# A hybrid decoder layer on one core: the sums over scale 2 and half of shift 2 move from the tensor engine to GpSimd

## The chip, the core and the metric

The kernel runs on one core of a Trainium2 chip. The core has a tensor engine (PE) for matrix products, VectorE (DVE) and ScalarE (ACT) for elementwise work, GpSimd (POOL), and a queue engine (SP) that here issues the loads. The engines run side by side, each through its own list of instructions in a fixed order, and wait for one another by semaphores. The metric is the device time of one execution in microseconds (us).

## The reference

One layer over 256 tokens of width 2048. A conditioning vector c gives six modulations through one large matrix; four token mixers share an input projection and an output projection; a gated feed-forward with a short convolution follows.

```python
cond = jax.nn.silu(c)
mod = (cond @ w_mod[l] + b_mod[l]).reshape(B, 6, D)
sh1, sc1, g1, sh2, sc2, g2 = [mod[:, i, None, :] for i in range(6)]

h = rmsnorm(x, norm_mix[l]) * (1.0 + sc1) + sh1
proj = f32(h @ w_in[l])
...
y = jnp.concatenate([y_a, y_b, y_c, y_d], axis=-1).astype(x.dtype) @ w_out[l]
x = x + g1 * y

h = rmsnorm(x, norm_ffn[l]) * (1.0 + sc2) + sh2
x = x + g2 * conv_ffn(h, ffn_w_gate[l], ffn_w_up[l], ffn_conv_w[l], ffn_conv_b[l], ffn_w_down[l])
```

The four mixers y_a to y_d are gated linear attention, gated DeltaNet, multi-scale pooling and forgetting attention. The change concerns the product `cond @ w_mod` for sc2 and the first half of sh2: a vector of 2048 times a 2048 x 1024 block of w_mod, three times.

## The kernel before

All is float32. A weight is loaded as a tile `wr` of 128x1024 (512 KB), split by ScalarE into a high part `wh` (L115) and by VectorE into a low part `wl` (L100, the difference), and the tensor engine makes three products of high and low parts where one full-precision product stands in the reference.

The modulations are matrix times vector, so they are made differently. w_mod is 2048 rows high; a load brings 128 rows of 1024 columns into a tile `wm`. There are 16 loads for each block of 1024 columns, a "job". The function `gemv` (L174) sums them in one of two ways:

- on VectorE: one instruction (L103) multiplies wm by the column of `cond` that belongs to the rows and adds into `ga`, 128x1024. After 16 loads, a product with a column of ones adds up the 128 partitions.
- on the tensor engine (`pst` is given): the column of `cond`, repeated over 32 columns, is the stationary operand, and wm streams through it in two halves of 512 (L193). Two loads and two halves fill four strips of 32 columns side by side, in one PSUM bank `bgt`. ScalarE copies the bank into a buffer of the tag wr (L201), and a product with `sel`, which holds ones in the rows 0 and 64, or 32 and 96, picks and adds the strips.

`gemv` is a generator: it yields after each two loads, a "step". L53 and L54 say which job goes which way: "s0 s1 h0" (both halves of scale 2, the first of shift 2) on the tensor engine, "h1 g0 g1" (the second half of shift 2, both halves of gate 1) on VectorE.

The stages around this are, in order:

- The modulations sh1 and sc1 and the input projection, in four groups of K tiles (to L527). The last group leaves 25 visits to pairs of column tiles (`extras`, L470).
- The mixers, with these last visits in between. At each visit, `paced` (L908) advances the tensor engine's jobs by 0.38 of a step and VectorE's by 0.69. So the loads of w_in and the loads of w_mod alternate. After the mixers' instructions, what is left of the jobs is written out, first those of the tensor engine, then those of VectorE (L940 to L943).
- The output projection (`project`, L950), which loads w_out, multiplies by gate 1 (`g1t`) and adds the residual.
- The second norm; scale 2 `s2` and shift 2 `sh2` enter at L1007. Then the feed-forward half (to L1088), where gate 2 is summed on VectorE as well.

The last step of a gate 1 job waits, in the order of writing, until the tensor engine's jobs are written out (L487). The buffers that the jobs share are four tiles of wm, whoever sums them; five of wr; and one bank bgt.

The code gives a priority by its order of writing; a planner puts the instructions of each engine in a fixed order, by this priority and its own estimate of when each can run, and within it the loads of SP. A load for which no buffer is free holds all loads behind it on SP. GpSimd runs few instructions: memsets (`ga` at L179, `Sg` at L813), twelve comparisons for masks (L393), and small powers for norms (L320, L577, L726, L839, L998, L1079).

Of the kernel before, what the change touches and what calls it, by code (L numbers as in the profile page):

```python
# [16 lines left out]
P = 128  # L17
# [11 lines left out]
# columns of w_in  # L29
# [3 lines left out]
# columns of the constant array  # L33
# [23 lines left out]
def _consts():  # L57
    i = np.arange(P)
    s, t = i[:, None], i[None, :]
    same = (s // CH) == (t // CH)  # L60
    cols = [s == t, same & (s <= t), same & (s > t), s <= t, np.ones((P, P)), s > t]
    cols.append(np.where(t > s, -1e30, 0.0))
    for w in (2, 4, 8, 16):
        cols.append(np.broadcast_to(1.0 / np.minimum(np.arange(1, 17), w), (P, 16)))
    # the level at which s and t part, counted from 1 above the diagonal and from 7 below it
    lv = sum((l + 1) * ((s // (2 * m) == t // (2 * m)) & (s % (2 * m) < m) & (t % (2 * m) >= m))
             for l, m in enumerate(LEVELS))
    lw = lv.T
    cols.append(lv + np.where(lw > 0, lw + len(LEVELS), 0))
    return np.ascontiguousarray(np.concatenate([np.asarray(a, np.float32) for a in cols], axis=1))  # L70
# [3 lines left out]
def trunk_kernel(ctx: ExitStack, tc: tile.TileContext, x, c, w_mod, b_mod, norm_mix, norm_ffn, w_in,  # L74
# [18 lines left out]
    def kt_(shape, name, dt=F32):  # L93
        return keep.tile(shape, dt, name=name, tag=name)
# [71 lines left out]
    last_wm = [None]  # L166
# [7 lines left out]
    def gemv(col0, done, pst=None, ready=lambda: True, bias=None):  # L174
        """cond * w over 1024 columns: without pst summed by partition on VectorE, else on the tensor engine,
        four column tiles side by side"""
        acc = pst() if pst else keep.tile([P, 1024], F32, name="ga", tag="ga")
        if bias is not None:
            G.memset(acc, 0.0)  # L179
            nc.sync.dma_start(acc[0:1], bias)  # L180
        for k in range(0, KT, 2):
            wms = []
            for kk in range(2):
                wms.append(wp.tile([P, 1024], F32, name="wm", tag="wm", bufs=4))
                last_wm[0] = nc.sync.dma_start(wms[kk], wm_v[:, k + kk, col0:col0 + 1024])
            for kk in range(2):
                wm = wms[kk]
                if not pst:
                    accumulate(acc, wm, k + kk, bias is None)
                    continue  # L190
                for c in range(2):
                    o = 64 * kk + 32 * c
                    mm(acc[o:o + 32], cond[:, k + kk:k + kk + 1].to_broadcast([P, 32]), wm[:, c * 512:c * 512 + 512],  # L193
                       start=k == 0, stop=k == KT - 2)
            if k == KT - 2:
                while not ready():
                    yield
                with tc.high_priority():
                    if pst:
                        gr = wp.tile([P, 1024], F32, name="wr", tag="wr", bufs=5)[:, 0:512]  # L200
                        S_.copy(gr, acc)  # L201
# [25 lines left out]
    # ================= attention half =================  # L227
    with ExitStack() as ph:
# [11 lines left out]
        # projections: gla q 0:2, k 2:4, g 4:8, gdn g 8:12, pool 12:16, fox q 16:20, k 20:24  # L240
# [16 lines left out]
        def gates():  # L257
# [13 lines left out]
            # columns 0:4 1/(1+e), columns 4:12 1/(2+e)  # L271
# [16 lines left out]
        with ExitStack() as st:  # L288
# [25 lines left out]
            # 1 + b_mod of the two scales  # L314
# [19 lines left out]
            # sh1, sc1 of the K tiles of group g, then h  # L334
# [60 lines left out]
            # the small columns: lr 0:16, b 16:20, a 20:24, f 24:28; row 28 is one  # L395
# [30 lines left out]
            # one pair of column tiles over some groups of K tiles; two sums share a bank: only the first clears it  # L426
# [49 lines left out]
            def jobs(seq, pst):  # L476
                col = pst or (ext)
                for job in seq.split():
                    kind, n = job[0], int(job[1])
                    k0, col0 = 8 * n, dict(s=4, h=3, g=2)[kind] * D + n * 1024  # L480
                    if kind == "s":
                        yield from gemv(col0, to_col(s2, 4, k0, nffn, col), pst)
                    elif kind == "h":
                        yield from gemv(col0, to_col(sh2, 3, k0, None, col), pst)
                    else:
                        yield from gemv(col0, g1_row(n, bgt), None,
                                        lambda: "gf"[n] in emitted and "s" in emitted, b_mod[:, col0:col0 + 1024])  # L487
# [7 lines left out]
            # g1 takes the place of values no longer needed  # L495
# [10 lines left out]
            bg = [marked(jobs(ON_PE, bgt)), jobs(ON_DVE, None)]  # L506
# [22 lines left out]
            # conv of gdn's q, k, v straight from the accumulators  # L529
# [16 lines left out]
        bgp = ph.enter_context(tc.tile_pool(name="bgp", bufs=1, space=PSUM))  # L546
        mx = ph.enter_context(ExitStack())
# [19 lines left out]
        def gated_deltanet():  # L567
            # norms of q and k
# [12 lines left out]
            # decays within the chunk  # L581
# [28 lines left out]
                # -M^T (and its diagonal, which no level takes)  # L610
# [9 lines left out]
            # inverse of I + M by blocks of 2, 4, .. 64: X = inverse, Y = its transpose  # L620
# [42 lines left out]
                # attention [j, i]  # L663
# [5 lines left out]
                # queries times the decay from the chunk's start  # L669
# [6 lines left out]
            # u and w^T, over the values' and the keys' place  # L676
# [10 lines left out]
            # the states, chunk by chunk, over M and X  # L687
# [34 lines left out]
                # r = c * (c^2 * ss / d + eps)^-1/2  # L722
# [17 lines left out]
        def gla(lp):  # L740
# [4 lines left out]
            # log decays by token, then their sums within the chunk by feature  # L745
# [14 lines left out]
            # attention within the chunk, [s, t], heads by parity: the diagonal, then level by level  # L760
# [29 lines left out]
            # to and from the states  # L790
# [16 lines left out]
            for cc in range(NC - 1):  # L807
# [4 lines left out]
                s = lt([P, 2, 256], "Sg", bufs=3)  # L812
# [93 lines left out]
        rate, owed = (PE_RATE, DVE_RATE), [0.0, 0.0]  # L906
# [81 lines left out]
    # ================= feed-forward half =================  # L988
    with ExitStack() as ph:
# [3 lines left out]
        with tc.tile_pool(name="hp", bufs=2, reuse_waits="tile") as hp:  # L993
# [7 lines left out]
            # transposed and scaled by the norm in one product  # L1001
# [12 lines left out]
        def proj(gp, view, c0):  # L1014
            """four column tiles, weights stationary: [features, tokens], the high and the low part's sums side by side"""
# [29 lines left out]
        # down: tokens stationary; g2 and the final norm's weight by row  # L1045
# [72 lines left out]
```

## Time and profile before

| | us |
|---|---|
| median of 3 runs | 1316.04 |
| lowest and highest run | 1313.96 and 1318.38 |
| span of the profiled execution, first to last instruction | 1312.4 |
| PE busy in it | 1257.7 |
| VectorE busy | 886.8 |
| ScalarE busy | 640.7 |
| GpSimd busy | 23.1 |

The profile is one execution; the page gives its span and no other time for it. The slices of the span, a fortieth each, show how the stages follow:

```profile
PE   2799999999999999899999999999999999999996
DVE  7688797989763497456656665665666587974553
POOL 0200000010000100000000000000000000000000
DMA  9999998796567996345565565555655699875552
```

Each digit is the busy share in tenths. The mixers lie in the slices 8 to 14, the output projection in 14 to 17; from there on it is the feed-forward half. A busy PE says little of how much it does: the ends of matmuls are modelled, and a matmul counts as busy while it passes through the array.

### The profile page before, as it was taken

To read this page: it belongs to the slowest core of one execution; us is meant where nothing else is said; L and a number is where in the kernel's file an instruction comes from. 1 tells how busy PE (TensorE), PEld (TensorE's weight loads), DVE (VectorE), ACT (ScalarE), POOL (GpSimd) and SP (SyncE) were. 2 spreads that over 40 slices of the span, in tenths; PEclk is the share of its full clock that TensorE was granted. 3 is DMA by queue.
4 is the path that set the end of the run, shared out by engine and by line. 5 is a ranking of instruction groups with operands and counts; after the bars stand their busy time and mean duration, and the time that the engine had idled before them with its cause. 6 is when DMAs were issued, how large, how long until landed. Compare 5 with 4: busy or idle time off the path is not lost.

```text
span 1312.4 us, 20435 instructions
## 1 busy us (share of the span) xinstructions
PE 1257.7 (96%) x7955; PEld 1100.5 (84%) x7955; DVE 886.8 (68%) x1185; ACT 640.7 (49%) x1008; POOL 23.1 (2%) x31
## 2 busy tenths in 40 slices
PE   2799999999999999899999999999999999999996
PEld 1799999898876788888888888888888888888896
DVE  7688797989763497456656665665666587974553
ACT  3455344674364444465545455554555454443432
POOL 0200000010000100000000000000000000000000
PEclk8799999999999999899999999999999999999998
DMA  9999998796567996345565565555655699875552
GB/s 332 287 368 376 312 353 279 259 334 211 176 233 247 328 338 230 125 161 186 170 206 180 189 190 183 190 184 187 191 184 172 206 356 378 304 260 188 192 182 81
DMA packets 174232, 311.95 MB, mean 238 GB/s; under 512 B 16172, under 2 KB 65331, under 8 KB 173495
## 3 DMA queue, kind: packets, MB, share of 16 engines
q1 hardware_dynamic: 174135, 310.65, 70.3%
q8 instruction: 62, 1.02, 0.3%
q14 instruction: 35, 0.29, 0.1%
HBM read 308.51 MB, written 2.10 MB: 237 GB/s over the span
## 4 chain that ended last, share of the span: by engine, by line
PE 91%; DMA 4%; DVE 1%; SPq 1%; ACT 1%; issue 1%; POOLq 0%; POOL 0%; ACTq 0%; DVEq 0%
PE fpt L97 57%; PE ext L97 15%; PE wot L97 5%; PE acc L97 4%; PE gdt L97 4%; PE bgt L97 3%; DMA wm<-in_w_mod_dram 3%; PE oxt L97 2%; DMA wr<-in_w_in_dram 1%; DMA wr<-in_w_out_dram 1%; DVE ga L103 1%; DVE wl L100 0%; ACT h L112 0%; SPq L155 0%; SPq L399 0%
## 5 line engine op out<-in xcount | busy, mean ns | idle before, releaser
L100 DVE TENSOR_TENSOR wl<-wr,wh 128x1024 fp32r<-128x1024 f32 x384 | 468.5, 1223 | 299.7 <-ACT wh L115 298.8
L115 ACT CAST wh<-wr 128x1024 fp32r<-128x1024 f32 x384 | 402.4, 1051 | 497.5 <-PE fpt L97 315.5
L97 PE MATMUL fpt<-bigA,wh 128*128 128x512 f32 x1408 | 485.0, 397 | 0.7 <-ACT h L112 0.7
L97 PE MATMUL fpt<-bigA,wl 128*128 128x256 f32 x1408 | 375.2, 281 | 0.0
L97 PEld LDWEIGHTS fpt<-bigA,wh 128*128 128x128 f32 x1408 | 260.9, 188 | 60.7 <-ACT h L112 0.9
L97 PEld LDWEIGHTS fpt<-bigA,wl 128*128 128x128 f32 x1408 | 259.5, 188 | 5.0
L103 DVE SCALAR_TENSOR_TENSOR ga<-wm,cond,ga 128x1024 f32<-128x1024 f32 x139 | 177.9, 1280 | 9.9 <-DMA wm<-in_w_mod_dram 8.7
L97 PE MATMUL fpt<-wl,AH 128*128 128x512 f32 (+1 forms) x440 | 152.9, 348 | 0.0
L97 PE MATMUL fpt<-wh,AL 128*128 128x512 f32 (+1 forms) x440 | 152.5, 347 | 0.0
L97 PE MATMUL fpt<-wh,AH 128*128 128x512 f32 (+1 forms) x440 | 142.6, 348 | 0.0
L97 PE MATMUL ext<-bigA,wh 128*128 128x256 f32 x768 | 137.9, 281 | 0.0
L97 PEld LDWEIGHTS ext<-bigA,wh 128*128 128x128 f32 x768 | 117.8, 189 | 3.1 <-DVE dS L100 0.8
L97 PE MATMUL ext<-bigA,wl 128*128 128x256 f32 x384 | 107.6, 281 | 1.7 <-DVE wl L100 1.7
L97 PEld LDWEIGHTS fpt<-wh,AH 128*128 128x128 f32 x440 | 83.3, 189 | 10.9 <-ACT wh L115 0.2
L97 PEld LDWEIGHTS fpt<-wh,AL 128*128 128x128 f32 x440 | 83.3, 189 | 10.5 <-issue 0.2
L97 PEld LDWEIGHTS fpt<-wl,AH 128*128 128x128 f32 x440 | 83.3, 189 | 10.5 <-issue 0.2
L97 PEld LDWEIGHTS ext<-bigA,wl 128*128 128x128 f32 x384 | 72.1, 188 | 3.0 <-DVE wl L100 2.1
L97 PE MATMUL acc<-bigA,wh 128*128 128x256 f32 x384 | 69.8, 288 | 4.6 <-ACT bigA L115 2.8
L97 PE MATMUL ext<-wh,bigA 128*128 128x256 f32 (+1 forms) x320 | 68.3, 305 | 0.0
L97 PEld LDWEIGHTS acc<-bigA,wh 128*128 128x128 f32 x384 | 60.1, 196 | 4.9 <-ACT bigA L115 2.9
L97 PE MATMUL wot<-wh,bigA 128*128 128x512 f32 (+1 forms) x256 | 63.0, 337 | 0.0
L97 PEld LDWEIGHTS ext<-wh,bigA 128*128 128x128 f32 x320 | 51.8, 188 | 5.5 <-ACT wh L115 1.7
(335 smaller groups left out, 1193.3 us busy)
## 6 DMA issues: line engine op xcount, KB each, us to landing
wm<-in_w_mod_dram SPq DMA_DIRECT2D x192, 512.0 KB, 6.0
wr<-in_w_in_dram SPq DMA_DIRECT2D x88, 512.0 KB, 9.6
wr<-in_ffn_w_gate_dram SPq DMA_DIRECT2D x88, 512.0 KB, 4.3
wr<-in_ffn_w_up_dram SPq DMA_DIRECT2D x88, 512.0 KB, 3.5
wr<-in_ffn_w_down_dram SPq DMA_DIRECT2D x88, 512.0 KB, 4.5
wr<-in_w_out_dram SPq DMA_DIRECT2D x32, 512.0 KB, 4.1
xt<-in_x_dram SPq DMA_DIRECT2D x2, 1024.0 KB, 7.0
bigC<-in_x_dram SPq DMA_DIRECT2D x2, 1024.0 KB, 11.3
```

The lines of the kernel that those rows point to most:

```text
L97: PE.matmul(o, lhsT=l, rhs=r, start=start, stop=stop, skip_group_check=True)
L100: V.tensor_tensor(out=o, in0=a, in1=b, op=op)
L103: V.scalar_tensor_tensor(out=o, in0=a, scalar=s, in1=b, op0=op0, op1=op1)
L115: S_.copy(hi, src)
```

## The change

The jobs "s0 s1 h0" are summed on GpSimd. [...] The sum is a `ga` of 128x1024 in a pool of its own, `bp`. The 128 partitions are then added up by products with ones, as for VectorE's jobs, in the bank bgt. `sel` goes. To make room for the new `ga`, the states `Sg` of gated linear attention for the first two chunks take the buffers of the tag `dd`. The rate of the jobs stays 0.38. Comments are dropped.

```diff
-# modulations (s: scale 2, h: shift 2, g: gate 1; half) summed on the tensor engine and on VectorE, steps per load of columns
-ON_PE, PE_RATE = "s0 s1 h0", 0.38
+
+ON_POOL, POOL_RATE = "s0 s1 h0", 0.38
 ON_DVE, DVE_RATE = "h1 g0 g1", 0.69
...
-    sel = kt_([P, 2], "sel")
-    V.memset(sel, 0.0)
-    for o in (0, 32, 64, 96):
-        V.memset(sel[o:o + 1, o // 32 % 2:o // 32 % 2 + 1], 1.0)
...
-    def accumulate(ga, src, k, first=True):
+    def accumulate(ga, src, k, first=True, on=V):
         if k == 0 and first:
-            tsc(ga, src, cond[:, k:k + 1], None, ALU.mult)
+            on.tensor_scalar(out=ga, in0=src, scalar1=cond[:, k:k + 1], scalar2=None, op0=ALU.mult)
+        elif on is V:
+            stt(ga, src, cond[:, k:k + 1], ga, ALU.mult, ALU.add)
         else:
-            stt(ga, src, cond[:, k:k + 1], ga, ALU.mult, ALU.add)
...
+            on.tensor_scalar(out=src, in0=src, scalar1=cond[:, k:k + 1], scalar2=None, op0=ALU.mult)
+            on.tensor_tensor(out=ga, in0=src, in1=ga, op=ALU.add)
...
-        acc = pst() if pst else keep.tile([P, 1024], F32, name="ga", tag="ga")
+    def gemv(col0, done, on=V, ready=lambda: True, bias=None):
+
+        acc = (keep if on is V else bp[0]).tile([P, 1024], F32, name="ga", tag="ga")
...
-                wm = wms[kk]
-                if not pst:
-                    accumulate(acc, wm, k + kk, bias is None)
-                    continue
-                for c in range(2):
-                    o = 64 * kk + 32 * c
-                    mm(acc[o:o + 32], cond[:, k + kk:k + kk + 1].to_broadcast([P, 32]), wm[:, c * 512:c * 512 + 512],
-                       start=k == 0, stop=k == KT - 2)
+                accumulate(acc, wms[kk], k + kk, bias is None, on)
...
-                    if pst:
-                        gr = wp.tile([P, 1024], F32, name="wr", tag="wr", bufs=5)[:, 0:512]
-                        S_.copy(gr, acc)
-                        done([(gr, sel[:, c:c + 1]) for c in range(2)])
-                    else:
-                        done([(acc[:, c * 512:c * 512 + 512], ones) for c in range(2)])
+                    done([(acc[:, c * 512:c * 512 + 512], ones) for c in range(2)])
...
-            bg = [marked(jobs(ON_PE, bgt)), jobs(ON_DVE, None)]
+            bg = [marked(jobs(ON_POOL, G, bgt)), jobs(ON_DVE, V, ext)]
...
+        bp[0] = ph.enter_context(tc.tile_pool(name="bp", bufs=1, reuse_waits="tile"))
...
-                s = lt([P, 2, 256], "Sg", bufs=3)
+
+                s = lt([P, 2, 256], "Sg", tag="dd", bufs=2) if cc < 2 else lt([P, 2, 256], "Sg")
...
-        rate, owed = (PE_RATE, DVE_RATE), [0.0, 0.0]
+        rate, owed = (POOL_RATE, DVE_RATE), [0.0, 0.0]
```

More of the change, by code (lines that the diff above doesn't have):

```diff
@@ L163, in load_split @@
         return wh, wl
-    last_wm = [None]
-    def accumulate(ga, src, k, first=True):
+    last_wm, bp = [None], [None]
+    def accumulate(ga, src, k, first=True, on=V):
         if k == 0 and first:
-            tsc(ga, src, cond[:, k:k + 1], None, ALU.mult)
-        else:
-            stt(ga, src, cond[:, k:k + 1], ga, ALU.mult, ALU.add)
-    def gemv(col0, done, pst=None, ready=lambda: True, bias=None):
-        acc = pst() if pst else keep.tile([P, 1024], F32, name="ga", tag="ga")
+            on.tensor_scalar(out=ga, in0=src, scalar1=cond[:, k:k + 1], scalar2=None, op0=ALU.mult)
+        elif on is V:
+            stt(ga, src, cond[:, k:k + 1], ga, ALU.mult, ALU.add)
+        else:
+            on.tensor_scalar(out=src, in0=src, scalar1=cond[:, k:k + 1], scalar2=None, op0=ALU.mult)
+            on.tensor_tensor(out=ga, in0=src, in1=ga, op=ALU.add)
+    def gemv(col0, done, on=V, ready=lambda: True, bias=None):
+        acc = (keep if on is V else bp[0]).tile([P, 1024], F32, name="ga", tag="ga")
         if bias is not None:
@@ L474, in extras, with jobs @@
                     done[p] = g + 1
-            def jobs(seq, pst):
-                col = pst or (ext)
+            def jobs(seq, on, col):
                 for job in seq.split():
@@ L481, in jobs @@
                     if kind == "s":
-                        yield from gemv(col0, to_col(s2, 4, k0, nffn, col), pst)
+                        yield from gemv(col0, to_col(s2, 4, k0, nffn, col), on)
                     elif kind == "h":
-                        yield from gemv(col0, to_col(sh2, 3, k0, None, col), pst)
+                        yield from gemv(col0, to_col(sh2, 3, k0, None, col), on)
                     else:
-                        yield from gemv(col0, g1_row(n, bgt), None,
+                        yield from gemv(col0, g1_row(n, bgt), on,
                                         lambda: "gf"[n] in emitted and "s" in emitted, b_mod[:, col0:col0 + 1024])
```

## The prediction

> **What bounds the kernel now.** I read the page's engine totals first, then its chain of work that ended last, then a table of busy time in three stretches, then the rows of the tiles that the change touches, and last the queue of SP.
>
> ```profile
> PE 1257.7 (96%) x7955; PEld 1100.5 (84%) x7955; DVE 886.8 (68%) x1185; ACT 640.7 (49%) x1008; POOL 23.1 (2%) x31
> 437.49 8.33 DMA wr<-in_w_out_dram
> 515.16 25.03 PE wot L97 x201
> 548.62 1.02 ACT h L112 x2
> 556.71 742.68 PE fpt L97 x4141
> ```
>
> The first line is the page's: the tensor engine is the busiest, GpSimd (POOL) nearly idle. The others are pieces of the chain in order of time. The feed-forward half is one unbroken run of matmuls from 556.71 us to the end; the change touches nothing in it, so it moves as a block. Scale 2 and shift 2 are first needed at 548.62, where L1007 writes h. All that can change lies ahead of that, behind 245 us, where the first strip matmul starts (row below). I cut it at 360 us, after which only three loads of w_in are left to split, and at 446, where the output projection starts.
>
> ```profile
> core 0: us, PE busy (x) PEld busy (x) DVE busy (x) ACT busy (x) POOL busy (x), PEclk, DMA share, GB/s
> 245.00:360.00 115.00, 114.40 (x934) 100.63 (x933) 98.27 (x152) 58.65 (x105) 4.73 (x2) 1.00 0.74 249
> 360.00:446.00 86.00, 86.00 (x602) 59.35 (x601) 37.69 (x92) 41.75 (x121) 3.02 (x3) 1.00 0.73 253
> 446.00:540.00 94.00, 93.58 (x503) 79.69 (x502) 72.00 (x78) 47.39 (x76) 3.71 (x3) 1.00 0.79 283
> ```
>
> Call them A, B and C. PE is full in all three. VectorE (DVE) is nearly full in A (98.27 of 115) and dense in C, and has room in B. The DMA engines are a quarter idle, and the clock was 1.00 throughout, so neither is a term below.
>
> **What is removed.** The stretches again, for the instructions that read the tile wm alone:
>
> ```profile
> core 0: us, PE busy (x) PEld busy (x) DVE busy (x), PEclk, DMA share, GB/s
> 245.00:360.00 115.00, 11.42 (x64) 1.75 (x64) 30.68 (x24) 1.00 0.74 249
> 360.00:446.00 86.00, 26.18 (x128) 4.09 (x128) 2.57 (x2) 1.00 0.73 253
> L97 PE MATMUL bgt<-wm,cond x192: 592/592/617, 245.2 to 436.5; 128*32 128x512 f32 x192
> L201 ACT COPY wr<-bgt x3: 586/586/587, 356.6 to 437.1; 128x512 f32<-128x512 f32 x3
> L97 PE MATMUL bgt<-sel,wr x48: 169/250/271, 360.4 to 441.8; 128*128 128x1 f32 x48
> L97 PE MATMUL ext<-ones,ga 128*128 128x1 f32 x80 | 11.0, 267 | 12.1 <-DVE ga L103 12.1
> ```
>
> The strips hold PE for 11.42 us in A (the first job, a third of the 192) and 26.18 us in B (the other two). The 48 column sums behind them stay: they read ga and ones where they read wr and sel, the same count at 267 ns for 250. The three ScalarE copies of L201 go; at 0.59 us each, with ScalarE under half busy, I count them at nothing.
>
> **What is added.** Three jobs of 16 loads: each load is one multiply by a scalar in place (the product overwrites wm) and, but for the first of a job, one add into a new ga; 48 multiplies and 45 adds of 128x1024 on GpSimd. The trace has no such operation. Nearest rows, all GpSimd:
>
> ```profile
> L179 POOL MEMSET ga<- 128x1024 f32 x4 | 3.8, 954 | 641.4 <-PE fpt L97 568.2 <-PE bgt L97 61.3 <-PE ext L97 11.8
> L813 POOL MEMSET Sg<- 128x512 f32 x3 | 1.5, 528 | 171.4 <-DVE bigA L100 171.4
> L393 POOL TENSOR_SCALAR mk<-ct 128x128 uint8<-128x128 f32 x12 | 6.9, 584 | 31.3 <-DMA ct<-in_cst_dram 30.7
> ```
>
> From below: a memset of the same shape, 0.95 us, which reads nothing. From above: the 128x128 compare taken eight times, 8 x 584 ns = 4.67 us. Between them I take a fixed part and a slope. The two memsets give (954 - 528) / 512 = 0.83 ns an element; the compare at that slope leaves 584 - 107 = 477 ns fixed. A multiply is then 0.48 + 0.85 = 1.33 us; an add reads two streams, so I double the slope: 0.48 + 1.70 = 2.18 us. One load costs 3.51 us, all of it 48 x 1.33 + 45 x 2.18 = 162 us. That GpSimd has the time (it is idle for 98%) doesn't settle it, because it doesn't work alone:
>
> ```profile
> 42.61 1.28 DVE L103 SCALAR_TENSOR_TENSOR ga<-wm,cond,ga 128x1024 f32<-128x1024 f32 x1
> 43.09 1.20 POOL L393 TENSOR_SCALAR mk<-ct 128x128 uint8<-128x128 f32 x1 [30.73 <-DMA ct<-in_cst_dram]
> 45.93 0.53 POOL L393 TENSOR_SCALAR mk<-ct 128x128 uint8<-128x128 f32 x1
> 450.91 1.21 DVE L100 TENSOR_TENSOR wl<-wr,wh 128x1024 fp32r<-128x1024 f32 x1
> 451.14 1.85 POOL L726 TENSOR_TENSOR oss<-oss,mhalf 128x4 f32<-128x4 f32 x1 [7.94 <-DVE oss L109]
> L839 POOL TENSOR_TENSOR ls<-ls,mhalf x2: 1007/1007/1007, 361.7 to 370.1; 128x4 f32<-128x4 f32 x2
> ```
>
> The compare takes 0.53 us, but 1.20 when it starts beside VectorE's sum into ga: VectorE ends at 43.89, the compare 0.40 us later. The power takes 1.007 us, but 1.85 beside VectorE's wl: it ends 0.87 us after it. Some 0.13 us of each ran meanwhile. So a GpSimd operation that reads SBUF waits for a VectorE operation that reads two SBUF tiles; I take it that the same holds the other way, and that the two add up. This is the term that decides. VectorE's demand of that kind, with the larger other forms of A (rows of A):
>
> ```profile
> L103 DVE SCALAR_TENSOR_TENSOR ga<-wm,cond,ga 128x1024 f32<-128x1024 f32 x24 | 30.7, 1279 | 1.2 <-DMA wm<-in_w_mod_dram 1.0
> L100 DVE TENSOR_TENSOR wl<-wr,wh 128x1024 fp32r<-128x1024 f32 x20 | 24.4, 1221 | 2.3 <-ACT wh L115 2.1
> L100 DVE TENSOR_TENSOR dd<-bT 128x512 f32<-128x512 f32 x6 | 4.0, 688 | 0.0
> L103 DVE SCALAR_TENSOR_TENSOR xt<-bigC,V,xt 128x253 f32<-128x253 f32 x8 | 3.7, 475 | 0.0
> L103 DVE SCALAR_TENSOR_TENSOR xt<-bigC,V,xt 128x254 f32<-128x254 f32 x8 | 3.6, 478 | 0.0
> L100 DVE TENSOR_TENSOR qE<-pr,E 128x256 f32<-128x256 f32 x6 | 2.6, 431 | 0.0
> ```
>
> **A.** 69 us of VectorE, 4.7 of GpSimd now, and the first job's 16 multiplies and 15 adds, 54 us: 127.7 us; less 0.13 x 31 = 4 for the part that needs no turn, 124, in a stretch of 115: **+9**. The 11.42 us that PE gains are worth nothing here, since PE then waits for wl.
>
> **B.** PE could fall by 26.18 to 59.8 us, but the mixers are chains through ScalarE and VectorE, and strips also fill their gaps. Neither end has a row; I take half, **-13**, so B is 73. The Trainium skill, in "Trainium Kernel Development and Optimization" (section Performance Expectations), calls matmul busy time a bad metric and weight-load busy time a good one; by the row of B, weight loads fill 59.35 of 86 us, so PE has slack already, and only the 4.09 us of the strips' own loads would come back, for 9 us more in the sum. No run here shows yet which is right.
>
> GpSimd in B has 73 less its 3.0 less VectorE's wl and ga (rows below and above: 3.66 and 2.57), 64 us, enough for 18 of the other 32 loads. 14 are left.
>
> ```profile
> 360.00:446.00 86.00, 6.88 (x24) 4.54 (x24) 3.66 (x3) 1.00 0.73 253
> 446.00:540.00 94.00, 56.30 (x159) 29.87 (x159) 41.39 (x34) 1.00 0.79 283
> 446.00:540.00 94.00, 0.00 (x0) 0.00 (x0) 20.44 (x16) 1.00 0.79 283
> ```
>
> **C.** wl 41.39 and ga 20.44 (the second half of gate 1, whose loads come behind GpSimd's in the four wm buffers), GpSimd's 3.7 and 14 x 3.51 = 49: 114.7; less 28 x 0.13, 111 in a stretch of 94: **+17**. The splits wl feed every output projection matmul, so PE waits with them.
>
> **The queue on POOL.** Five small powers, and memsets, now stand behind multiplies and adds: the ones at L577 and L726 lie on DeltaNet's chain. Each waits for what runs, on average half an operation, 0.9 us: three are **+3**. Behind a power that waits for VectorE the sums wait too, but nobody needs them before 548.62.
>
> **The queue on SP.** A wm buffer is held 3.51 us a load where now the 30 of B pass in 56 us, 1.9 each:
>
> ```profile
> 381.41 56.02 SPq L185 DMA_DIRECT2D wm<-in_w_mod_dram  x30
> 437.49 5.01 SPq L155 DMA_DIRECT2D wr<-in_w_out_dram  x5
> ```
>
> The w_out loads stand right behind them. If that order stays, the projection starts later; if the slower releases let w_out pass first, its 8.33 us wait on the chain goes. I put this at 0 and keep both signs in the range.
>
> Sum: +9 - 13 + 17 + 3 = +16 on a span of 1312.4 us. The page gives no time of its own beside the span; the median of the runs is 3.6 above it, so I put the change on the median: 1316 + 16 = **1332 us**. In "SBUF — State Buffer" (section "SBUF: two separate sides") the Trainium skill has the shared pair of ports held for the whole instruction, the loser fully blocked; by that, without my 0.13, A and C are 4 us longer each, 1340. The two waits above agree with the blocking, not quite with "whole".
>
> **Rivals.**
> 1. *The engines don't share a turn, or GpSimd is quick* (**faster**). Then PE's relief comes through: -11.4 in A, -13 in B: 1316 - 24 = 1292. For it: PE is full everywhere, and only two waits of that kind are in the trace. Against: in both, GpSimd's end follows VectorE's. It decides in C: 94 - 41.4 - 20.4 - 3.7 = 28.5 us hold 28 operations only if one costs 1.0 us.
> 2. *It cancels*: PE's 24 us against A and C at a third of their overrun; 1316, within 4 us.
> 3. *Backlog on POOL*: the order on POOL is fixed beforehand, and if the 14 loads stand ahead of the power of L726, DeltaNet waits 49 us for its norm: 1316 - 13 + 49 = 1352, or 1361 with A's 9.
> 4. *The price is the upper bound*: 93 x 4.67 = 434 us from 245 reach 679; needed at 548.62: +130, 1446. It decides from (548.6 - 245 - 11.5) / 93 = 3.1 us an operation.
>
> **How the numbers follow.** Forecast case 0.45, with its own range 1321 to 1350 (half the overrun, or the whole-instruction lock without B's gain); rival 1 0.24; rival 2 0.10; rival 3 0.15; rival 4 0.06. A measurement here can't tell less than about 0.3%, 4 us, from no change. Slower: 0.45 + 0.15 + 0.06 = 0.66; within: 0.10; faster: 0.24. The range 1298 to 1380 leaves out about half of rival 1 and all of rival 4.
>
> **What would show it.** Right: GpSimd busy some 160 to 220 us between 245 and 540, adds near 2.2 us and longer beside wl; wl and ga on VectorE above 1.22 and 1.28 us on average; idle time of PE put down to wl; the projection later than 446. Wrong: GpSimd's multiplies and adds below 1 us; wl unchanged at 1.22 and the first fpt matmul on wh ahead of 556.71 (rival 1); a long wait of VectorE or ScalarE for oss (rival 3); h waiting for scale 2 (rival 4).

## The result, and the profile after

| | before | after |
|---|---|---|
| median | 1315.48 us (4 runs) | 1420.36 us (4 runs, 1418.07 to 1424.47) |
| ratio of the runs | | 1.080 [1.0778, 1.0822] |
| span of the profiled execution | 1312.4 | 1422.6 |
| mean granted clock of PE | 0.985 | 0.935 |

The kernel became 105 us slower. The forecast was 1332 with a range to 1380: the sign holds, the size doesn't, and the time lies outside the range. The engine totals and three of the slice rows of the changed kernel's page:

```profile
PE 1251.1 (88%) x7763; PEld 1114.3 (78%) x7763; DVE 939.2 (66%) x1180; ACT 640.3 (45%) x1005; POOL 288.5 (20%) x124
PE   2899999949789893158999999999999999999996
POOL 0200011466789769700000000000000000000000
PEclk8799999968989897568999999999999999999998
```

PE's row has two holes where before there was none: a shallow one while the mixers run (slices 9 to 14) and a deep one in slices 16 to 18, in the first two of which POOL is at 9 and 7 tenths while PE is at 3 and 1; the granted clock falls with it. The same stretches A, B and C as in the prediction, and the one behind them, by the view of busy time by stretch (the columns are named in its second line):

```profile
core 0: us, PE busy (x) PEld busy (x) DVE busy (x) ACT busy (x) POOL busy (x), PEclk, DMA share, GB/s
245.00:360.00 115.00, 91.67 (x700) 87.60 (x701) 96.89 (x128) 54.24 (x92) 63.62 (x25) 0.85 0.66 208
360.00:446.00 86.00, 73.54 (x510) 65.60 (x509) 74.36 (x104) 41.97 (x97) 69.75 (x25) 0.92 0.64 206
446.00:540.00 94.00, 86.70 (x441) 71.59 (x440) 52.71 (x61) 39.15 (x84) 74.47 (x29) 0.95 0.57 194
540.00:667.00 127.00, 49.57 (x287) 42.15 (x286) 46.05 (x59) 24.32 (x51) 60.05 (x26) 0.65 0.45 149
```

PE works 23 us less in A than before (91.67 for 114.40), and 77 of 127 us behind C are empty. The chain of work that ended last, from where GpSimd carries it (start, length, what):

```profile
595.24 2.35 POOL ga L170
597.63 3.59 PE bgt L97 x16
601.47 2.09 PE bgt L97 x2
...
630.66 4.92 DMA wm<-in_w_mod_dram
...
638.33 2.09 PE bgt L97 x2
...
643.15 7.56 PE wot L97 x57
...
666.88 742.67 PE fpt L97 x4141
```

From 531 to 597.63 us the chain is GpSimd's multiplies and adds, one behind the other. Then come the column sums of shift 2 (x16), the first row of gate 1 (601.47), the loads of gate 1's second half with VectorE's sums, its row (638.33), the last products of the output projection (wot) and the feed-forward run. That run has the length that it had, 742.67 for 742.68 us; it starts 110 us later. Three of the waits of all engines between 230 and 700 us, and GpSimd's own groups:

```profile
ACT gv L197 <- PE bgt L97: 61.2, 1, 61.2
...
POOL wm L169 <- DMA wm<-in_w_mod_dram: 54.9, 10, 12.6
...
PE bgt L97 <- POOL ga L170: 52.1, 1, 52.1
```

```profile
L169 POOL TENSOR_SCALAR wm<-wm,cond x45: 2835/2844/5135, 205.4 to 587.6; 128x1024 f32<-128x1024 f32 x45
L170 POOL TENSOR_TENSOR ga<-wm,ga x45: 2331/2377/3427, 266.9 to 595.2; 128x1024 f32<-128x1024 f32 x45
```

PE stood 52.1 us at one instruction, a column sum of shift 2, because the sum wasn't there; what writes gate 1's first row (gv) waits behind the same instruction. In the second fence, three numbers are the shortest, median and longest duration in ns; the shortest stand here for an operation left alone: a multiply takes 2.84 us and an add 2.33. 48 and 45 of them are 241 us undisturbed.

### The profile page after: what moved, and what is told of

Its sections match the earlier page's. It is cut to its first block, busy times and chain, and to the rows that moved or that the text cites. A ratio compares the mean times of both kernels' runs of the same rounds, so it can differ in the third digit from the quotient of the medians.

```text
span 1422.6 us, 20155 instructions
## 1 busy us (share of the span) xinstructions
PE 1251.1 (88%) x7763; PEld 1114.3 (78%) x7763; DVE 939.2 (66%) x1180; ACT 640.3 (45%) x1005; POOL 288.5 (20%) x124
## 4 chain that ended last, share of the span: by engine, by line
PE 73%; DVE 10%; DMA 6%; POOL 5%; ACT 2%; issue 2%; SPq 1%; POOLq 0%; ACTq 0%; DVEq 0%
PE fpt L97 52%; PE ext L97 11%; DMA wm<-in_w_mod_dram 5%; DVE ga L103 3%; PE acc L97 3%; PE wot L97 3%; POOL wm L169 3%; PE gdt L97 2%; POOL ga L170 2%; DVE wl L100 2%; PE bgt L97 1%; PE oxt L97 1%; DVE xt L103 1%; ACT wh L115 1%; DMA wr<-in_w_in_dram 1%
## 5 line engine op out<-in xcount | busy, mean ns | idle before, releaser
L100 DVE TENSOR_TENSOR wl<-wr,wh 128x1024 fp32r<-128x1024 f32 x384 | 485.6, 1269 | 305.9 <-ACT wh L115 297.5
L103 DVE SCALAR_TENSOR_TENSOR ga<-wm,cond,ga 128x1024 f32<-128x1024 f32 x139 | 184.1, 1325 | 22.2 <-DMA wm<-in_w_mod_dram 21.0
L169 POOL TENSOR_SCALAR wm<-wm,cond 128x1024 f32<-128x1024 f32 x45 | 141.1, 3140 | 241.0 <-DMA wm<-in_w_mod_dram 208.2
L176 POOL MEMSET ga<- 128x1024 f32 x4 | 3.8, 951 | 612.6 <-PE fpt L97 567.9
L170 POOL TENSOR_TENSOR ga<-wm,ga 128x1024 f32<-128x1024 f32 x45 | 117.6, 2613 | 0.9
L97 PE MATMUL ext<-wh,bigA 128*128 128x256 f32 (+1 forms) x320 | 73.5, 319 | 2.1 <-DVE bigA L100 1.0
```

Source lines behind the costliest of these rows:

```text
L97: PE.matmul(o, lhsT=l, rhs=r, start=start, stop=stop, skip_group_check=True)
L100: V.tensor_tensor(out=o, in0=a, in1=b, op=op)
L103: V.scalar_tensor_tensor(out=o, in0=a, scalar=s, in1=b, op0=op0, op1=op1)
L169: on.tensor_scalar(out=src, in0=src, scalar1=cond[:, k:k + 1], scalar2=None, op0=ALU.mult)
L170: on.tensor_tensor(out=ga, in0=src, in1=ga, op=ALU.add)
```

## The experiments

Two theories stood after the result. **Length**: the sums are too long for the time there is, and what waits for the last of them is late. **Turns**: GpSimd and VectorE block each other when both read SBUF, which makes the mixers late and GpSimd longer. A third cost, gate 1 written behind GpSimd's jobs, could be added to either. All kernels below are the changed one with an edit, if nothing else is said; the scheduler orders the other instructions anew for each, so differences of a few us are not read as an effect. Where the times of two kernels from different sessions are compared, the ratio to before is the better measure, since before was run anew in each.

**GpSimd busy as long, but reading nothing.**

```diff
-            on.tensor_scalar(out=src, in0=src, scalar1=cond[:, k:k + 1], scalar2=None, op0=ALU.mult)
-            on.tensor_tensor(out=ga, in0=src, in1=ga, op=ALU.add)
+            for _ in range(3):
+                on.memset(src, 0.0)
+            for n in (1024, 1024, 400):
+                on.memset(ga[:, 0:n], 0.0)
...
```

The first load of a job gets three memsets of wm and one of ga.

> GpSimd's multiplies and adds are replaced by memsets of about the same length (three of 0.95 us for a multiply of 2.84 us, 0.95 + 0.95 + 0.43 for an add of 2.33 us) on the same tiles, so they read nothing from SBUF; the sums over scale 2 and half of shift 2 are left out. Theory P (the length of GpSimd's chain, 48 loads of 5.17 us, sets when the jobs end, and what waits for them follows): the chain keeps its length but for some 26 us of stretching, the last job ends near 575 instead of 598, time 1385 to 1410. Theory L (VectorE and GpSimd block each other at SBUF, the prediction's term): the mixers lose their delay too (first power of DeltaNet's norm back from 474 to about 445), wl back to 1.22 us, time below 1365.

Measured: 1344.6 us, ratio 1.0191 [1.0152, 1.0231]. Its chain, and VectorE's two groups between 245 and 540 us in this kernel:

```profile
517.06 0.96 POOL ga L177
518.55 3.59 PE bgt L97 x16
...
587.59 742.66 PE fpt L97 x4141
```

```profile
L100 DVE TENSOR_TENSOR wl<-wr,wh 128x1024 fp32r<-128x1024 f32 x53 | 64.7, 1221 | 36.7 <-ACT wh L115 36.5
L103 DVE SCALAR_TENSOR_TENSOR ga<-wm,cond,ga 128x1024 f32<-128x1024 f32 x27 | 34.6, 1281 | 4.0 <-DMA ga<-in_b_mod_dram 3.4 <-DMA wm<-in_w_mod_dram 0.7
```

VectorE's operations are back at their durations of before (1221 and 1279). The column sums behind GpSimd's last operation start 79 us earlier (518.55 for 597.63), and from there to the feed-forward run it is 69 us in both kernels. So the end of GpSimd's work is passed on to the end of the kernel one to one, and three quarters of the loss hang on what GpSimd reads. About a third of the 79 us is the longer operations of GpSimd itself (267 us for the 243 of the memsets); more of it is waits of GpSimd for loads of wm, from 245 us to its last operation 54.9 us in the changed kernel and 11.4 here.

**Gate 1 written ahead of GpSimd's jobs.**

```diff
-                                        lambda: "gf"[n] in emitted and "s" in emitted, b_mod[:, col0:col0 + 1024])
+                                        lambda: "gf"[n] in emitted, b_mod[:, col0:col0 + 1024])
...
-            for b_ in bg:
+            for b_ in bg[::-1]:
```

> The same work; what is left of the jobs after the mixers is written out with VectorE's jobs (gate 1) ahead of GpSimd's, and the last step of a gate 1 job no longer waits for GpSimd's jobs. Theory O (the cost lies in gate 1, which stands behind GpSimd's last job: its row at 601, its second half at 638, the feed-forward half at 667): gate 1 is done by about 500, only scale 2 and shift 2 are late, the feed-forward half starts some 15 us after the last sum on GpSimd, near 612, time 1360 to 1375. Theory P with no part in O: GpSimd's end sets all, 1410 to 1425. Theory L: no difference, 1420.

Measured: 1403.9 us, ratio 1.0641 [1.06, 1.0682], so 21 us less by the ratios (16 by the times), and not the 45 to 60 expected. Its chain:

```profile
633.45 3.57 PE bgt L97 x16
637.02 751.66 PE fpt L97 x4205
```

Gate 1 is out of the chain: the feed-forward follows the column sums at once, where it took 69 us. But the loads now reach VectorE's jobs first, and GpSimd's last sum ends at 633 instead of 598. What one part gains the other loses.

**Both edits together.**

> Both changes of the earlier two runs together: GpSimd writes for as long as the sums took but reads nothing (the sums are left out), and gate 1's jobs are no longer written behind GpSimd's. Theory 'two parts' (turns with VectorE, and gate 1 in a row behind the last sum): both are gone, so the mixers end as in the run that reads nothing (ls near 382, oss near 436 to 440), GpSimd ends at 515 to 535, the first fpt matmul on wh is at 555 to 570, the time 1313 to 1330. Rival 'something common' (buffers of wm held longer, another order of the loads): the time stays at 1338 to 1350 as with the reads alone taken away.

Measured: 1324.8 us, ratio 1.0077 [1.0044, 1.0110]. The four kernels give a table of the loss against before, each from its own ratio:

| | gate 1 behind GpSimd | gate 1 ahead |
|---|---|---|
| GpSimd reads | +105 | +84 |
| GpSimd reads nothing | +25 | +10 |

Reading costs 74 to 80 us, the order 15 to 21. The last 10 are length: here too the feed-forward follows GpSimd's last operation directly, 3.6 us behind it:

```profile
553.95 0.96 POOL ga L177
555.44 3.57 PE bgt L97 x16
559.02 751.87 PE fpt L97 x4205
```

**The removal alone.** GpSimd clears ga once a job in place of the sums; loads and column sums stay.

```diff
...
+                on.memset(ga, 0.0)
...
-            on.tensor_scalar(out=src, in0=src, scalar1=cond[:, k:k + 1], scalar2=None, op0=ALU.mult)
-            on.tensor_tensor(out=ga, in0=src, in1=ga, op=ALU.add)
+            pass
```

> The removal alone: the changed kernel with all its loads of w_mod and its column sums, but GpSimd only clears ga at the start of a job; the 48 multiplies and 45 adds are left out. It prices the tensor engine's relief of 37.6 us of strips. The prediction had -13 us in its forecast, -24 in the rival where the relief comes through whole: 1292 to 1305. Rival 'no bound' (the mixers are chains and the strips filled gaps): 1310 to 1320.

Measured: 1315.1 us, ratio 0.9992 [0.9980, 1.0003]. Taking 37.6 us of strips from PE brings nothing here: with this order of instructions, even sums at no cost would not have made the kernel faster. The run prices the removal together with what came of it: the loads of w_mod, which no sum on GpSimd holds up now, come earlier (DMA share 0.93 in A, 0.74 before), and the first power of ls stands at 380.95 us for 361.66. That is 19 us late with no sum on GpSimd, and it costs nothing at the end.

**Half the columns** (the operations take 512 of 1024 columns).

```diff
-            on.tensor_scalar(out=src, in0=src, scalar1=cond[:, k:k + 1], scalar2=None, op0=ALU.mult)
-            on.tensor_tensor(out=ga, in0=src, in1=ga, op=ALU.add)
+            on.tensor_scalar(out=src[:, 0:512], in0=src[:, 0:512], scalar1=cond[:, k:k + 1], scalar2=None, op0=ALU.mult)
+            on.tensor_tensor(out=ga[:, 0:512], in0=src[:, 0:512], in1=ga[:, 0:512], op=ALU.add)
```

> GpSimd multiplies and adds only 512 of the 1024 columns of each load; the other half of the sums is left out. Theory P: the price of a load falls to about 2.6 us, the chain to 125 us, it ends with the mixers, and the time falls to 1290 to 1330. Theory L: the turns at SBUF halve as well, and with the sum of stretches A and C at 170 us of VectorE's and 80 of GpSimd's the overrun of the mixers (some 30 us) falls to about 10: not below 1320. Theory O alone: the order of the queues is the same, gate 1 still behind, above 1340.

Measured: 1333.2 us, ratio 1.0104 [1.0061, 1.0148]. GpSimd's groups in it:

```profile
L169 POOL TENSOR_SCALAR wm<-wm,cond 128x512 f32<-128x512 f32 x45 | 93.5, 2080 | 232.4 <-DMA wm<-in_w_mod_dram 189.3 <-DVE z L103 25.1 <-issue 6.9
L170 POOL TENSOR_TENSOR ga<-wm,ga 128x512 f32<-128x512 f32 x45 | 64.9, 1443 | 1.5
```

With the three first multiplies of full width, 9.1 us, they are busy 167.5 us, turns included, close to the 162 us that the prediction gave the whole change; the last column sums come at 491 us, and PE waits no more than 4.2 us for any. With work of the size that was forecast, the kernel takes the time that was forecast, 1332, just above what the theory of length allowed here. The total agrees better than the parts: the first power of ls is 21 us late (382.6 for 361.7), where the prediction put A at +9.

**The price of the multiply.** Once with an immediate in place of the column of cond, once as a `tensor_tensor` with the column broadcast.

```diff
-            on.tensor_scalar(out=src, in0=src, scalar1=cond[:, k:k + 1], scalar2=None, op0=ALU.mult)
+            on.tensor_scalar(out=src, in0=src, scalar1=0.5, scalar2=None, op0=ALU.mult)
```

> The 45 multiplies on GpSimd take an immediate 0.5 in place of a column of cond (so the sums are of half the weights, cond left out of them). Question: why a multiply (2.84 us) is dearer than an add with two inputs (2.33 us). Theory 'scalar': the column read for each partition makes it dear; then an undisturbed multiply falls to 1.4 to 2.0 us, the sums end about 40 us earlier and the time is 1365 to 1395. Rival 'operation': the form of instruction costs 2.84 us whatever its scalar; undisturbed multiply 2.8 to 2.9 us, time 1410 to 1430.

```diff
-            on.tensor_scalar(out=src, in0=src, scalar1=cond[:, k:k + 1], scalar2=None, op0=ALU.mult)
+            on.tensor_tensor(out=src, in0=src, in1=cond[:, k:k + 1].to_broadcast([P, 1024]), op=ALU.mult)
```

> GpSimd's multiplies but for a job's first are made by the two-input form, with the column of cond repeated along the row as the second input. Theory P: if the two-input form costs 2.33 us whatever it computes, 45 x 0.5 = 23 us less of GpSimd's chain, time 1395 to 1400. If the scalar from SBUF is not what makes the multiply slow: 2.8 us, 1420. Theory L: the second input is one more reader, more blocking, 1420 to 1435.

Measured: 1421.3 us (one run) and 1405.8 us, ratio 1.0655 [1.0603, 1.0707]. The multiplies of the two, in this order:

```profile
L169 POOL TENSOR_SCALAR wm<-wm x45: 2762/2775/3872, 202.8 to 585.2; 128x1024 f32<-128x1024 f32 x45
```

```profile
L169 POOL TENSOR_TENSOR wm<-wm,cond x45: 1887/2412/3067, 204.4 to 561.8; 128x1024 f32<-128x1024 f32 x45
```

The column of scalars isn't what makes it dear: 2.78 us without it. The form of instruction is: as `tensor_tensor` the same product takes 1.89 us at best, less than the 2.33 expected. That saves GpSimd 33 us of multiplies (107.7 for 141.1), of which its adds give back 10 (127.6 for 117.6), and the kernel is faster than the changed one by 19 us by the ratios (15 by the times).

**Own buffers.** Two of the four wm buffers for GpSimd's loads, two for VectorE's.

```diff
-                wms.append(wp.tile([P, 1024], F32, name="wm", tag="wm", bufs=4))
+                wt = "wm" if on is V else "wg"
+                wms.append(wp.tile([P, 1024], F32, name=wt, tag=wt, bufs=2 if bp[0] is not None else 4))
```

> The changed kernel with two of the four wm buffers for GpSimd's loads alone and two for VectorE's (the loads ahead of the mixers keep four). Theory 'starved' (GpSimd waits for loads whose buffers VectorE's jobs hold, some 43 us between 245 and 486): GpSimd's last sum ends 25 us or more earlier than 597.6, time 1375 to 1400. Rival 'turns': the waits only move, GpSimd is held by VectorE's turns and its own price; last sum within 15 us of 597.6, time 1405 to 1435.

Measured: 1454.0 us, ratio 1.1049 [1.1020, 1.1078], above both expectations. GpSimd waits 63.4 us for loads where it waited 54.9, and the last sum ends at 608. So two buffers of its own don't shorten its waits; more were not tried. Not all of the loss lies there: the edit leaves two buffers to gate 2 in the feed-forward half as well, and there VectorE's sums wait 23.7 us for loads from 1150 us on, where they waited 2.5.

**One job of three on GpSimd.** Three kernels made from the kernel before: scale 2 stays in strips on PE, only "h0" (16 loads) goes to GpSimd, and gate 1 doesn't wait for it. The first has its loads late and its column sums in the banks ext; the second has the loads three times as densely, so early; the third is the first with the column sums in the bank bgt. (Its added condition on "s" changes nothing: the jobs of scale 2 are written out ahead of GpSimd's in all three.)

```diff
-ON_PE, PE_RATE = "s0 s1 h0", 0.38
+ON_PE, PE_RATE = "s0 s1", 0.25
+ON_POOL, POOL_RATE = "h0", 0.13
...
-            bg = [marked(jobs(ON_PE, bgt)), jobs(ON_DVE, None)]
+            bg = [marked(jobs(ON_PE, bgt)), jobs(ON_DVE, None), jobs(ON_POOL, None, G)]
```

> The kernel before with the first half of shift 2 alone on GpSimd (16 loads, some 83 us of it undisturbed), scale 2 still in strips on the tensor engine, gate 1 not behind GpSimd. Theory 'turns cost by the load': a third of the loss to turns (76 us by the run without reads), 25 us, less a third of the strips' 37.6 us of PE, at most 12: 1316 to 1335 us, not faster than before by more than 5 us. Rival 'only the late end costs': GpSimd is done before 500, nothing waits for it, PE is relieved: 1300 to 1311 us. GpSimd's multiply 2.8 to 3.2 us and add 2.3 to 2.7 us in both; wl on VectorE above 1.24 us by the first, 1.22 to 1.23 by the second.

```diff
-ON_POOL, POOL_RATE = "h0", 0.13
+ON_POOL, POOL_RATE = "h0", 0.4
```

> As the kernel with one job of 16 loads on GpSimd, but these loads are written three times as densely, so that GpSimd is done before the mixers end and no column sum is late. What is left is turns with VectorE and the tensor engine's relief (a third of the strips, 12.5 us of PE). Theory 'late end' (of the 74 us that the one job cost, the 48 us in which PE stood at its column sums, and what they held up, were nearly all): 1312 to 1330 us. Rival 'turns': a third of 76 us stays, with the mixers' ends 10 us late or more: 1335 to 1350.

```diff
-                        yield from gemv(col0, to_col(sh2, 3, k0, None, col), pst, on=on)
+                        yield from gemv(col0, to_col(sh2, 3, k0, None, col if on is V else bgt), pst, ready=(lambda: True) if on is V else (lambda: "s" in emitted), on=on)
```

> As the kernel with one job of 16 loads on GpSimd late, but its column sums take the bank bgt in place of one of the two ext banks, in which the first columns of the output projection are summed. Theory 'bank': PE's 48 us at those column sums held up the projection only because it needs the ext banks behind them; then 1335 to 1355 us, and the projection starts before 480. Rival 'order': PE's instructions stand in the same order whatever the bank, 1380 to 1395.

| one job on GpSimd | us | ratio |
|---|---|---|
| late, column sums in ext | 1389.7 | 1.0549 [1.0525, 1.0574] |
| early, column sums in ext | 1341.1 | 1.0186 [1.0166, 1.0207] |
| late, column sums in bgt | 1318.5 | 1.0008 [0.9996, 1.0020] |

The same work on the same engine costs 72, 24 or 1 us. In the first, PE's waits between 446 and 540 us read:

```profile
PE ext L98 <- POOL ga L176: 47.7, 1, 47.7
```

The output projection's first columns are summed in the two ext banks, behind the column sums of GpSimd's job; 16 loads of GpSimd hold up all of it, which both expectations for this kernel missed. With bgt the wait is gone, though GpSimd's last sum ends even later (546 us for 522): the gain is larger than the 35 to 55 us that the theory of the bank allowed.

The second kernel has no late sum and still loses 24 us. Its time lies in the range of 'turns', and its mixers end late, as that theory says. But the third kernel shows that this is not what costs. The first power for oss, on DeltaNet's chain, and the first load of w_out on the chain of work that ended last, in the second kernel, then in the third:

```profile
458.17 1.04 POOL L731 TENSOR_TENSOR oss<-oss,mhalf 128x4 f32<-128x4 f32 x1 [66.77 <-DVE oss L110]
465.34 11.00 DMA wr<-in_w_out_dram
```

```profile
459.62 1.96 POOL L731 TENSOR_TENSOR oss<-oss,mhalf 128x4 f32<-128x4 f32 x1 [23.89 <-DVE oss L110]
418.76 7.59 DMA wr<-in_w_out_dram
```

The mixers' norm is 16 to 17 us later than before (442.19) in both. The loads of w_out differ: they come 28 us later than before (437.49) in the second kernel, behind the loads of the strips, which last until 464 us there and until 418 in the third. With 2.7 us more for the load itself that is about what the two profiled spans differ by (1341.6 for 1312.4). In the third kernel the projection's products start at 427 us and fill the gaps of the late mixers. Why the strips are late in the second kernel, by the denser loads ahead of them or by GpSimd's slow release of the four wm buffers, isn't separated. Here are A of the second and C of the third:

```profile
245.00:360.00 115.00, 101.23 (x742) 89.03 (x741) 100.29 (x137) 54.05 (x95) 77.09 (x27) 0.90 0.75 242
```

```profile
446.00:540.00 94.00, 91.07 (x501) 77.12 (x500) 73.96 (x79) 44.05 (x86) 65.95 (x22) 0.98 0.84 285
```

77 us of GpSimd in A, beside the mixers, go with 13 us less of PE (101.23 for 114.40). 66 us of it in C, beside the output projection, go with 2.5 less (91.07 for 93.58), though wl is stretched there from 1.22 to 1.65 us on average.

**The other way round**, from the kernel before: VectorE's job "h1" goes to PE too, since strips were free.

```diff
-ON_PE, PE_RATE = "s0 s1 h0", 0.38
-ON_DVE, DVE_RATE = "h1 g0 g1", 0.69
+ON_PE, PE_RATE = "s0 s1 h0 h1", 0.5
+ON_DVE, DVE_RATE = "g0 g1", 0.46
```

> The opposite direction, from the kernel before: the second half of shift 2, which VectorE sums there (16 operations of 1.28 us, 20.5 us), goes to the tensor engine's strips as the other three jobs; GpSimd stays as it was. Theory 'tensor engine has slack' (taking 37.6 us of strips away brought 1.7 us or nothing): 12.5 us more of strips cost nothing, VectorE is freed of 20.5 us in the stretch 245 to 360 where it was busy 98 of 115 us: 1300 to 1312 us. Rival 'order': the strips' own waits in the tensor engine's queue eat it, 1314 to 1322.

Measured: 1353.7 us, ratio 1.0291 [1.0272, 1.0310]; both expectations missed. The strips now last until 479 us, and the first load of w_out on the chain comes at 479.63 (before 437.49), behind their loads. That strips take no time on PE doesn't mean that their loads take none on SP. No kernel of these beats the one before.

## Why the prediction was wrong in size

**Price (3.51 us a load, 162 us in all): the step that failed.** The multiply was put at 1.33 us from the slope of a memset, on the thought that one input stream costs what one output stream does. It takes 2.84, more than the add, which was put at 2.18 and takes 2.33. A load is 5.17 us, all of it 241 undisturbed and 267 as run. The upper bound, 4.67 an operation, was as far off, so the memset was the wrong neighbour and no row stood near. With 5.17 in the prediction's own sum, A holds 69 + 4.7 + 80.4 - 4, or +35; 12 loads fit in B, so C gets 20 and comes to +70; with -13, and +4 for the queue, the sum is +96, that is 1412. The half-width kernel shows the reverse: work of 167 us gives 1333. In the prediction's own sum most of the miss is this one term. That 1412 comes so near to 1420 is luck in part: the sum has no term for the order of gate 1, and its parts don't all agree with the runs, as the next paragraphs show.

**Turns: the mechanism held, the way of adding up didn't.** This is VectorE against GpSimd in A of the changed kernel:

```profile
304.94 4.82 POOL L170 TENSOR_TENSOR ga<-wm,ga 128x1024 f32<-128x1024 f32 x2
```

```profile
304.38 0.68 DVE L100 TENSOR_TENSOR dd<-bT 128x512 f32<-128x512 f32 x1
304.98 2.59 DVE L100 TENSOR_TENSOR E<-pr,E 128x256 f32<-128x256 f32 x1
307.49 2.82 DVE L100 TENSOR_TENSOR dd<-bT 128x512 f32<-128x512 f32 x1
```

Two adds of 2.34 and 2.40 us follow each other without a gap. The small E (0.41 us alone) takes 2.59 and ends 0.29 us after the first of them; dd, 0.68 a moment before, takes 2.82 and ends 0.55 after the second. So it does hold both ways, which the trace of before couldn't show. By groups between 245 and 540 us, before and then after:

```profile
L636 DVE COPY_PREDICATED W<-mk,gdt 128x512 f32<-128x512 uint8 x10 | 7.3, 730 | 0.8 <-PE gdt L97 0.6
L100 DVE TENSOR_TENSOR bigA<-pr,bigA 128x256 fp32r<-128x256 f32 x16 | 6.2, 419 | 5.2 <-ACT bigA L115 5.1
```

```profile
L100 DVE TENSOR_TENSOR wl<-wr,wh 128x1024 fp32r<-128x1024 f32 x49 | 77.2, 1581 | 30.7 <-ACT wh L115 23.2 <-PE ext L97 7.3
L103 DVE SCALAR_TENSOR_TENSOR ga<-wm,cond,ga 128x1024 f32<-128x1024 f32 x26 | 39.4, 1516 | 8.1 <-DMA wm<-in_w_mod_dram 8.0
L100 DVE TENSOR_TENSOR bigA<-pr,bigA 128x256 fp32r<-128x256 f32 x16 | 9.6, 632 | 1.8 <-ACT bigA L115 1.6
L621 DVE COPY_PREDICATED W<-mk,gdt 128x512 f32<-128x512 uint8 x10 | 7.3, 727 | 1.8 <-PE gdt L97 1.7
```

wl, ga and bigA, which take two inputs from SBUF, are stretched; W, whose second input is in PSUM, is not. The rule of the Trainium skill on this ("SBUF — State Buffer", section "SBUF: two separate sides": the pair of ports is held for the whole instruction, the loser blocked) agrees with the small E, which waited for nearly all of the add. Not quite all: by the two ends, 0.12 and 0.13 us of E and dd ran meanwhile, the 0.13 that the prediction took off for each operation.

The way of adding up is not confirmed. With the measured price the sum gives A +35, and in the changed kernel the first power of ls does come 36 us late (397.84 for 361.66); but 19 us of lateness are there without any sums, in the kernel of the removal alone. And the path to PE was wrong. The prediction let PE wait for wl. Between 245 and 540 us PE waits 1.9 us for wl in the changed kernel, and longer for single small operations of the mixers on VectorE:

```profile
PE gdt L603 <- DVE nbrk L103: 8.2, 1, 8.2
...
PE ext L97 <- DVE wl L100: 1.9, 4, 0.6
```

Nor does a late stretch by itself make the kernel late. By the sum, with the operations that the traces show in each stretch, one job early in A (11 multiplies and 11 adds of it there, 57 us) and one late in C (10 and 10, 52 us) would cost about 13 and 9 us; they cost 24 and 1, the first through w_out's loads. Adding up engine time also says nothing of GpSimd's own idle time: from 245 to 597.63 us it is busy 265 of 353 us, and the other 87 it waits, 54.9 for loads of wm and 23.9 for ScalarE's work in bigC before a first sum.

**B, -13, and rival 1's -24:** nothing; the removal alone is worth 1 us by its ratio, 2.6 at most by the interval. Here the doubt that the Trainium skill gave ("Trainium Kernel Development and Optimization", Performance Expectations: weight-load busy time, not matmul busy time, says how near PE is to its limit) agrees with the run: by the 4 us of the strips' weight loads in B little could come back, and next to nothing did. In the sum the 13 us hardly mattered: a B of 86 us has room for 22 loads of 3.51 us in place of 18, C falls from +17 to +4, and the total stays +16. For the same reason the 9 us that the prediction added for that doubt would have been given back in C.

**C, and "nobody needs them before 548.62", said of the sums: wrong.** The sums' own reader, h, could wait until then. But gate 1's last step was written behind GpSimd's jobs (the condition on "s", L487 of the kernel before), its rows use the same bank bgt, and PE takes its list in order. So all that follows needs the last sum at a point that moves with it: 69 us of gate 1 and output projection stood behind 597.63. The order is worth 15 to 21 us, by the table of four. The prediction named gate 1's second half behind GpSimd in the wm buffers, and gave that wait no price.

**The queue on POOL, +3, and rival 3:** the first power for ls waited 3.2 us behind a multiply (its input ended at 394.66, it started at 397.84), the two for oss 1.2 and 0.2. So the small term was about right (4.6 us in all), and no backlog stood before the norm; it was 32 us late (474.28 for 442.19) because its input was.

**The queue on SP, 0:** of its two signs the changed kernel shows the second. The first load of w_out is issued at 364.21 us, ahead of most of GpSimd's loads, and the projection's first product stands at 423.56 (447.06 before); what that was worth can't be read apart. Two other kernels show the first sign, and what it can cost: w_out's loads 28 us later with one early job (24 us in all) and 42 us later with h1 on PE (38 us in all).

**Rival 4** had the right end, the last sums late, with the wrong condition. Its 3.1 us an operation holds for a GpSimd that never pauses; the mean was 2.87 us, and the 87 us of pauses did the rest.

**Its signs:** GpSimd busy 208 us in A to C (160 to 220 expected), adds at 2.33, wl and ga stretched: these came true, and fit a loss of 16 us as well as one of 105. Two did not: PE's idle time isn't put down to wl, and the projection starts earlier, not later; its end is late. The sign that told was the one filed under rival 4, a wait of the last readers for the sums.

## What to carry to other kernels

Before work goes to an idle engine, find the price of exactly that instruction on that engine (a short kernel with it would do), and list what is written behind its result: a bank, a queue or an order can make a cheap sum cost 72 us or 1. An engine that is busy 96% may have nothing to give back; take the work out and look before counting its time as gain. Before a delay is priced, look at what loads are written behind it: mixers some 16 us late cost 24 us where w_out's loads came late as well, and 1 us where these came early and their products filled the gaps.

## What the hardware showed unexpectedly

- On GpSimd a multiply by a scalar, with one input, is slower than an add with two: 2.84 us and 2.33 for 128x1024. At 128x512 the shortest are 1.55 and 1.26, so an element costs some 2.5 and 2.1 ns, against 0.83 for a memset. With an immediate the multiply takes 2.78, as a product with a broadcast column 1.89.
- GpSimd's memsets, which read nothing, don't stretch VectorE: wl at 1221 ns on average between 245 and 540 us, with GpSimd busy 230 of the 295 us (83.28 of 86 in B).
- Operations of VectorE with a single, tiny input from SBUF were held as well, each beside an add: cq, 128x8, 0.16 us before and 2.30 in the changed kernel, and one on oss, 128x4, 2.12 us where the same took 0.17 a moment before.
- In the kernel without reads and with gate 1 ahead, seven operations of VectorE in a row, cq the first, are shown as ending together near 300.1 us, after up to 8.79 us, with only memsets running on GpSimd. Nothing in the trace explains it, and cq takes no more than 2.3 us in any other profile.
- While PE waited, its granted clock fell to 0.65 (540 to 667 us), and the products with ga for gate 1's rows took 1.06 to 1.22 us each, where they took 0.59 before.
